# Block compression's first layer by three products of 256 columns for even and odd blocks in place of two of 512

## The chip, the cores and the metric

The kernel runs on one core of one Trainium2 chip. The metric is the device time of one execution in microseconds (us), the median of several runs. Engines are named as in the profile: PE (TensorE; PEld is its loading of weights), DVE (VectorE), ACT (ScalarE), POOL (GpSimd), SP (SyncE, which issues most DMAs).

## What is computed

One inference step of a hybrid decoder layer for 512 prompt tokens and 64 sample tokens (8 requests of 8 tokens, each with 1024 cached rows): an input projection, three mixers, an output projection, a feed-forward part, all in fp32. The change concerns the third mixer's compression of key and value rows to blocks:

```
def compress_blocks(rows, pos_emb, w1, w2):      # CMP_BLOCK 32, CMP_STRIDE 16, CMP_HIDDEN 128
    chunks = rows.reshape(bsz, n_chunks, CMP_STRIDE, g, dh)
    blocks = jnp.concatenate([chunks[:, k:k + n_blocks] for k in range(CMP_SPAN)], axis=2)
    blocks = blocks + pos_emb[:, None, :]
    flat = jnp.transpose(blocks, (0, 1, 3, 2, 4)).reshape(bsz, n_blocks, g, CMP_BLOCK * dh)
    return jax.nn.gelu(flat @ w1) @ w2
```

A block is two neighbouring chunks of 16 rows, so block n is W0 times chunk n plus W1 times chunk n+1, where W0 and W1 are the upper and the lower half of `w1` (1024 x 128 each). It is done for keys (`src` 0) and for values (`src` 1), with 4 heads.

## The kernel before

**Products.** A product in fp32 is made as three products in float32r: each operand is split into a high part (a rounded copy, made by ACT at L93) and a low part (the difference, made by DVE at L96), and high·high, high·low and low·high are added up in PSUM.

**The main stream.** `run_group` (products at L424) runs through the input projection in jobs of 128 output columns: 16 k tiles a job, and 6 products of 288 columns a k tile (`pg<-hhi,whi`, `pg<-hlo,whi`, `pg<-hhi,wlo`, each for two halves of the 576 tokens). Weights are loaded by SP (`raw<-in_w_in`, 256 KB each) and split into `whi` (ACT) and `wlo` (DVE). When a job ends, DVE multiplies the accumulated `pg` into a tile `u` that the job's own tasks then finish (`norm_T` with two fp32 products against `bones`, `kv_finish` with transposes into the staging tiles `tk` and `tks`).

**The side work.** Everything else is in generators that a `Pump` steps through. After each k tile `pump.run` gives it 369 ns per half; each product or transpose that a task issues adds an assumed price (for float32r the larger of 107 ns and columns/2.4 ns). A scheduler then orders the instructions of each engine. The chain of tasks is `compress(0)`, `compress(1)`, then, when the projection's key, value and query jobs are finished, the attention of the sample tokens and of the prompt.

**The compression.** `compress(src)` has 40 units (u, J): for u = 0 to 3 two of the eight requests, 128 rows of chunks (512 columns with the 4 heads), for u = 4 the prompt (32 rows, 128 columns); J = 0 to 7 takes two of a chunk's 16 rows, which is one k tile of W0 and one of W1. A unit's rows are gathered by POOL (`cr`), then `turn(i)` makes them ready: DVE copies them to `by_g` (L692, one buffer), PE transposes four pieces into a tile of `pt` (L124), ACT makes `xh` from it, DVE makes `xl`. Two pairs of `xh` and `xl` take turns. The unit's products follow, two for each of three pairs (weights, rows), where W1's read the rows shifted by one column:

```
            for half in range(2):
                k = half * 8 + J
                for w, x in ((w1h, xh), (w1h, xl), (w1l, xh)):
                    mm(pa[:, :n], w[:, k, :], x[:, half:half + n], start=(J == 0 and first),
                       stop=(J == 7 and half == 1 and w is w1l))
```

They add up in `pa`, the one buffer of `po`. `turn(i + 1)` is issued ahead of the products of unit i. After J = 7 a task `tail` does the rest: `gelu2` with the positions' share `hb` as bias, the second layer and, for keys, a norm (`k_cmp_norm`, with an inverse root `kcr` on POOL). PSUM has three buffers of `pt`, one of `po` and two of `pg`.

**The positions' share.** `prep_w1(src)` loads `w1` in four pieces (`w1r`), splits it into `w1h` and `w1l`, and multiplies each of its 16 k tiles in fp32 by a column of `cols2` (the positions): 16 products, of two records each, with one output row of 128. `compress` copies the row (`hr`) and turns it into the column `hb` by one fp32 product against ones.

Of the kernel before, what the change touches and what calls it, by code (L numbers as in the profile page):

```python
# [76 lines left out]
def hybrid_step_kernel(ctx, tc, x_prompt, x_sample, cache_k, cache_v, cache_win_k, cache_win_v,  # L77
# [11 lines left out]
    def dram(t, off, ap):  # L89
        return bass.AP(tensor=t.tensor, offset=t.offset + off, ap=ap)  # L90
# [67 lines left out]
    def po(name="po"):  # L158
        return psum.tile([128, 512], F32, name=name, tag="o", bufs=1)
# [315 lines left out]
    def kv_finish(br, kv, p, u):  # L475
# [107 lines left out]
    w1, hbs = {}, {}  # L583

    def prep_w1(src):
        w1h = cpool.tile([128, 16, 128], F32R, name="w1h", tag="w1h", bufs=1)
        w1l = cpool.tile([128, 16, 128], F32R, name="w1l", tag="w1l", bufs=1)
        pb = hbs[src] = po()
        for c in range(4):
            raw = cpool.tile([128, 4, 128], F32, name="w1r", tag="cr", bufs=6)  # L590
            nc.sync.dma_start(raw, dram(cmp_w1, src * 2048 * 128 + c * 512 * 128, [[128, 128], [128 * 128, 4], [1, 128]]))
# [4 lines left out]
        w1[src] = w1h, w1l  # L596

    def begin(ci):
        if ci == 1:
# [36 lines left out]

    t1g, t1 = open_pool("t1", side="right")

    def gelu2(hid, pa, hb, n):

        hx = t1.tile([128, 512], F32, name="hx", tag="hx", bufs=1)
        act(hx[:, :n], pa[:, :n], AF.Identity, bias=hb)
        t_ = t1.tile([128, 512], F32, name="ht", tag="ht", bufs=1)
        act(t_[:, :n], pa[:, :n], AF.Square, bias=hb)
        stt(t_[:, :n], t_[:, :n], 1.0 / 0.044715, hx[:, :n], OP.add, OP.mult)
        act(t_[:, :n], t_[:, :n], AF.Tanh, scale=0.7978845608028654 * 0.044715)
        stt(hid[:, :n], t_[:, :n], 1.0, hx[:, :n], OP.add, OP.mult)

    def k_cmp_norm(pc, n):

        kc = t1.tile([128, 256], F32, name="kcn", tag="kcn", bufs=1)
        act(kc[:n], pc[:n, :256])
        sq = t1.tile([128, 256], F32, name="kcs", tag="kcs", bufs=1)
        tt(sq[:n], kc[:n], kc[:n], OP.mult)
        r4 = t1.tile([128, 4], F32, name="kcr", tag="kcr", bufs=1)
        V.reduce_sum(r4[:n], sq[:n].rearrange("p (g d) -> p g d", g=4), axis=AX)
        rsqrt_small(r4[:n], 1.0 / 64)
        tt(kc[:n].rearrange("p (g d) -> p g d", g=4), kc[:n].rearrange("p (g d) -> p g d", g=4),
           r4[:n, :, None].to_broadcast([n, 4, 64]), OP.mult)
        return kc  # L660

    def compress(src):
# [10 lines left out]
        hr = t1.tile([1, 128], F32, name="hr", tag="hr", bufs=1)  # L673
        V.tensor_copy(hr, hbs[src][:1, :128])
        yield
        ps = pt()
        mm(ps[:, :1], hr, ones[:1, :1], start=True, stop=True)
        V.tensor_copy(hb, ps[:, :1])
        pa = None
        X = {}  # L680
        xhl = [[t1.tile([128, 514], F32R, name=f"{n}{k}", tag=f"{n}{k}", bufs=1) for n in ("xh", "xl")] for k in range(2)]
        for t_ in xhl[0] + xhl[1]:
            V.memset(t_[:, 512:514].bitcast(F32), 0.0)

        def turn(i):
            u, J = units[i]
# [9 lines left out]
            act(xh[:, :n], ps[:, :n])  # L696
            tt(xl[:, :n], ps[:, :n], xh[:, :n], OP.subtract)
            if u == 4:
                V.memset(xh[:, n:n + 2].bitcast(F32), 0.0)
                V.memset(xl[:, n:n + 2].bitcast(F32), 0.0)  # L700
            X[i] = (xh, xl)

        for i, (u, J) in enumerate(units):
# [21 lines left out]
            first = True  # L725
            for half in range(2):
                k = half * 8 + J
                for w, x in ((w1h, xh), (w1h, xl), (w1l, xh)):
                    mm(pa[:, :n], w[:, k, :], x[:, half:half + n], start=(J == 0 and first),
                       stop=(J == 7 and half == 1 and w is w1l))  # L730
                    first = False
            yield
            if J < 7:
                continue
            done["tail"] += 1
            pump.add(tail(src, u, n, pa, hb, w2), front=True)
            yield

    def tail(src, u, n, pa, hb, w2):

        gk = cols[:, R_KN:R_KN + 1]
        hid = t1.tile([128, 512], F32, name="hid", tag="hid", bufs=1)
        gelu2(hid, pa, hb, n)
        for _ in range(TY):
            yield
        pc = pt()
# [1206 lines left out]
```

## Time and profile before

| | |
|---|---|
| median of 3 runs | 2938.94 us (2937.56 to 2941.04) |
| profiled execution | 2934.84 us, its span 2933.0 us |
| mean granted clock of PE | 0.994 of full speed |
| PE busy | 2860.9 us (98%) |
| DVE, ACT, POOL busy | 1867.9 (64%), 1157.9 (39%), 585.7 us (20%) |

The span is the profiled part of one execution; the device time of that execution is 1.84 us longer, and 4.10 us below the median of the runs. Busy shares are means over stages with different limits. PE's rows overlap, since a product's row reaches to its modelled end: the price of a product in a stream is the distance from start to start.

### The profile page before, as it was taken

To read this page: it belongs to the slowest core of one execution; us is meant where nothing else is said; L and a number is where in the kernel's file an instruction comes from. 1 tells how busy PE (TensorE), PEld (TensorE's weight loads), DVE (VectorE), ACT (ScalarE), POOL (GpSimd) and SP (SyncE) were. 2 spreads that over 40 slices of the span, in tenths; PEclk is the share of its full clock that TensorE was granted. 3 is DMA by queue.
4 is the path that set the end of the run, shared out by engine and by line. 5 is a ranking of instruction groups with operands and counts; after the bars stand their busy time and mean duration, and the time that the engine had idled before them with its cause. 6 is when DMAs were issued, how large, how long until landed. Compare 5 with 4: busy or idle time off the path is not lost.

```text
span 2933.0 us, 56799 instructions
## 1 busy us (share of the span) xinstructions
PE 2860.9 (98%) x22226; PEld 2739.6 (93%) x22226; DVE 1867.9 (64%) x3790; ACT 1157.9 (39%) x2140; POOL 585.7 (20%) x630
## 2 busy tenths in 40 slices
PE   7999999999999999998999999999999999999999
PEld 6998999888788898998999999999999999999999
DVE  5454445566877747577998888888888753343332
ACT  4353344333555423354544444444444431222222
POOL 3526321664443202033111101101101000000000
PEclk9999999999999999999999999999999999999999
DMA  7434344775231154475553333333333272333333
GB/s 229 126 107 137 103 104 105 223 221 131 60 76 41 50 174 120 132 212 155 174 165 110 110 102 110 111 103 116 100 113 110 79 240 82 116 113 90 89 100 95
DMA packets 467796, 361.94 MB, mean 123 GB/s; under 512 B 64553, under 2 KB 428048, under 8 KB 467528
## 3 DMA queue, kind: packets, MB, share of 16 engines
q1 hardware_dynamic: 443800, 297.89, 34.3%
q0 software_dynamic: 20944, 55.13, 6.5%
q10 hardware_dynamic: 2784, 5.29, 0.5%
q8 instruction: 175, 2.87, 0.4%
q14 instruction: 93, 0.76, 0.1%
HBM read 305.51 MB, written 50.61 MB: 121 GB/s over the span
## 4 chain that ended last, share of the span: by engine, by line
PE 57%; DVE 2%; DMA 1%; issue 1%; ACT 0%; POOL 0%; ACTq 0%; POOLq 0%; DVEq 0%
PE pg L424 24%; PE pg L1833 18%; PE pt L1833 9%; PE po L1833 5%; DVE wlo L96 1%; PE pt L124 1%; PE pt L120 1%; PE pt L424 0%; DVE x L105 0%; DVE X L96 0%; DMA u<-g_d 0%; DVE x L96 0%; DMA raw<-in_w_up_dram 0%; PE po L120 0%; DVE raw L96 0%
## 5 line engine op out<-in xcount | busy, mean ns | idle before, releaser
L93 ACT ACTIVATE whi<-raw 128x512 fp32r<-128x512 f32 x729 | 458.0, 630 | 975.5 <-PE pg L424 673.8
L96 DVE TENSOR_TENSOR wlo<-raw,whi 128x512 fp32r<-128x512 f32 x729 | 506.9, 696 | 398.7 <-ACT whi L93 373.8
L424 PE MATMUL pg<-ghl,whi 128*128 128x288 f32 x2816 | 495.4, 297 | 8.9 <-ACT ghl L93 8.6
L424 PEld LDWEIGHTS pg<-ghl,whi 128*128 128x128 f32 x2816 | 415.2, 189 | 9.9 <-ACT ghl L93 9.0
L424 PE MATMUL pg<-hhi,whi 128*128 128x288 f32 (+1 forms) x1440 | 336.1, 312 | 6.4 <-DVE u L96 4.7
L424 PE MATMUL pg<-hlo,whi 128*128 128x288 f32 (+1 forms) x1440 | 319.6, 300 | 1.1 <-DVE hlo L105 1.1
L424 PE MATMUL pg<-hhi,wlo 128*128 128x288 f32 (+1 forms) x1440 | 314.2, 299 | 0.3 <-DVE wlo L96 0.3
L424 PE MATMUL pg<-ghl,wlo 128*128 128x288 f32 x1408 | 302.3, 296 | 0.0
L424 PEld LDWEIGHTS pg<-hhi,whi 128*128 128x128 f32 (+1 forms) x1440 | 235.0, 190 | 28.5 <-issue 14.3
L1833 PE MATMUL pt<-X,fhi 128*128 128x288 f32 x1280 | 258.5, 296 | 0.0
L1833 PE MATMUL pg<-X,fhi 128*128 128x288 f32 x1232 | 246.7, 294 | 0.0
L424 PEld LDWEIGHTS pg<-hlo,whi 128*128 128x128 f32 (+1 forms) x1440 | 233.4, 189 | 6.3 <-issue 3.1
L424 PEld LDWEIGHTS pg<-hhi,wlo 128*128 128x128 f32 (+1 forms) x1440 | 232.7, 189 | 3.0 <-issue 2.2
L96 POOL TENSOR_TENSOR u<-u 128x576 f32<-128x576 f32 x44 | 69.7, 1584 | 823.8 <-DVE u L96 756.5
L424 PEld LDWEIGHTS pg<-ghl,wlo 128*128 128x128 f32 x1408 | 226.0, 189 | 0.0
L93 ACT ACTIVATE fhi<-wr 128x512 fp32r<-128x512 f32 x225 | 142.2, 632 | 189.4 <-PE pt L1833 107.1
L96 DVE TENSOR_TENSOR flo<-wr,fhi 128x512 fp32r<-128x512 f32 x225 | 197.5, 878 | 13.9 <-ACT fhi L93 11.4
L1833 PEld LDWEIGHTS pt<-X,fhi 128*128 128x128 f32 x1280 | 205.8, 188 | 0.0
L1833 PEld LDWEIGHTS pg<-X,fhi 128*128 128x128 f32 x1232 | 197.8, 188 | 0.0
L424 PE MATMUL pg<-S,whi 128*128 128x288 f32 x1024 | 195.5, 298 | 0.0
L1833 PE MATMUL pt<-X,flo 128*128 128x288 f32 x640 | 189.2, 296 | 0.0
L96 DVE TENSOR_TENSOR x1T<-pg,x1T 128x576 f32<-128x576 f32 x96 | 72.6, 757 | 180.6 <-PE pg L424 180.6
(1308 smaller groups left out, 5756.7 us busy)
## 6 DMA issues: line engine op xcount, KB each, us to landing
wr<-in_w_gate_dram SPq DMA_DIRECT2D x88, 512.0 KB
wr<-in_w_up_dram SPq DMA_DIRECT2D x88, 512.0 KB
raw<-in_w_down_dram SPq DMA_DIRECT2D x176, 256.0 KB
raw<-in_w_in_dram SPq DMA_DIRECT2D x144, 256.0 KB
raw<-in_w_out_dram SPq DMA_DIRECT2D x64, 256.0 KB
g_d<-u POOLq DMA_DIRECT2D x44, 288.0 KB
u<-g_d SPq DMA_DIRECT2D x44, 288.0 KB
raw<-in_w_in_dram SPq DMA_DIRECT2D x64, 128.0 KB
```

Of the source, the lines that this page charges most:

```text
L93: S.activation(out, in_, func, bias=bias, scale=scale, accum_out=accum)
L96: (eng or V).tensor_tensor(out, a, b, op=op)
L120: PE.matmul(out, lhsT, rhs, start=start, stop=stop, skip_group_check=True, **kw)
L124: PE.transpose(out, in_, ident)
L424: PE.matmul(ps[:m, s, :HALF], w[:, k, :m], x[:, s * HALF:(s + 1) * HALF], start=(k0 + k == 0 and n == 0), stop=(k0 + k == n_k - 1 and n == 2))
L1833: PE.matmul(P[n], w[:, k, :], xx, start=(j == 0 and q_ == 0), stop=(j == 7 and q_ == 2))
```

## The change

For u < 4 the blocks are taken in pairs. With chunk n of a unit written as x(n), the block at an even place 2m is W0·x(2m) + W1·x(2m+1), which is W0·(x(2m) − x(2m+1)) + (W0+W1)·x(2m+1); the block at the odd place is W1·(x(2m+2) − x(2m+1)) + (W0+W1)·x(2m+1). So three products of 256 columns stand for two of 512, each still three times for the split parts: 9 products of 256 columns a unit where there were 6 of 512. Of the parts that serve this:

- `turn` for u < 4: from the transposed rows in `pt` ACT copies the odd columns into a new tile `by_d` (256 columns); DVE writes the differences even − odd (256 and 255 columns) to it; ACT makes `xh` in two pieces (256 odd columns straight from `pt`, 511 differences from `by_d`), DVE makes `xl` in the same two pieces. `by_d` shares the one buffer of `by_g`, so the next unit's `by_g` comes behind this unit's last `xl`.
- Products: `pa` collects W0's and W1's parts in its two halves, `pb` the shared part with `wsh` and `wsl` (W0+W1, split). `pb` is a tile of `pt`, held for the eight units of one u.
- `compress` loads the pieces of `w1` a second time (four more loads of 256 KB for each `src`, by SP), adds W0 and W1 on DVE and splits the sum.
- The positions' share: 32 products of two columns for each `src` (`w1h` against the high and low part of the positions, `w1l` against the high part and zero), in place of the fp32 products; DVE adds the two columns to `hb`.
- To make room: `tk` and `tks` get one buffer in place of two; `gelu2` works in `hid` and `hx` alone (an addition on DVE brings in `pb`), and `k_cmp_norm` uses the buffers of `hx` and `hid`.

For u = 4 the six products of 128 columns remain. The diff, cut to its core:

```diff
-            stage[br, kv] = [t1.tile([128, 4, 256], F32, name="tk", tag="tk", bufs=2),
-                             t1.tile([TS, 256], F32, name="tks", tag="tks", bufs=2) if not (kv and br) else Vs[:, br - 1, :], 0]
+            stage[br, kv] = [t1.tile([128, 4, 256], F32, name="tk", tag="tk", bufs=1),
+                             t1.tile([TS, 256], F32, name="tks", tag="tks", bufs=1) if not (kv and br) else Vs[:, br - 1, :], 0]
...
-        pb = hbs[src] = po()
...
-            for k in range(4):
-                j = 4 * c + k
-                mm(pb[:1, :128], cols2[:, src * 16 + j:src * 16 + j + 1], raw[:, k, :], start=(j == 0), stop=(j == 15))
...
+        if pb is None:
+            act(hx[:, :n], pa[:, :n], AF.Identity, bias=hb)
+        else:
+            act(hid[:, :256], pb[:, :256], AF.Identity, bias=hb)
+            tt(hx.rearrange("p (n e) -> p e n", e=2), pa.rearrange("p (e n) -> p e n", e=2),
+               hid[:, None, :256].to_broadcast([128, 2, 256]), OP.add)
...
-        mm(ps[:, :1], hr, ones[:1, :1], start=True, stop=True)
...
+        for c in range(2):
+            a, b = [cpool.tile([128, 4, 128], F32, name="w1r", tag="cr", bufs=6) for _ in range(2)]
+            w1_in(a, src, c)
+            w1_in(b, src, c + 2)
+            yield
+            yield
+            tt(a, a, b, OP.add)
+            split(wsh[:, 4 * c:4 * c + 4], wsl[:, 4 * c:4 * c + 4], a)
         ps = pt()
+        for j in range(16):
+            mm(ps[:, :2], w1h[:, j, :], pos[:, j, 0:2], start=(j == 0), stop=False)
+            mm(ps[:, :2], w1l[:, j, :], pos[:, j, 2:4], start=False, stop=(j == 15))
+        V.reduce_sum(hb, ps[:, :2], axis=AX)
...
+                eo = ps.rearrange("p (n e) -> p e n", e=2)
+                d_ = t1.tile([128, 512], F32, name="by_d", tag="by_g", bufs=1)
+                act(d_[:, 256:], eo[:, 1])
+                tt(d_[:, :256], eo[:, 0], d_[:, 256:], OP.subtract)
+                tt(d_[:, 256:511], eo[:, 0, 1:], d_[:, 256:511], OP.subtract)
+                act(xh[:, 512:], eo[:, 1])
+                act(xh[:, :511], d_[:, :511])
+                tt(xl[:, 512:], eo[:, 1], xh[:, 512:].bitcast(F32), OP.subtract)
+                tt(xl[:, :511], d_[:, :511], xh[:, :511].bitcast(F32), OP.subtract)
...
-                pa = po()
+                pa, pb = po(), pt() if u < 4 else None
...
+                for w_, k, out, x0 in (((w1h, w1l), J, pa[:, :256], 0), ((w1h, w1l), 8 + J, pa[:, 256:512], 256),
+                                       ((wsh, wsl), J, pb[:, :256], 512)):
+                    for n_, (w, x) in enumerate(((w_[0], xh), (w_[0], xl), (w_[1], xh))):
+                        mm(out, w[:, k, :], x[:, x0:x0 + 256], start=(J == 0 and n_ == 0 and x0 != 256),
+                           stop=(J == 7 and n_ == 2))
```

How the instructions stand on PE now. Before, a unit of the compression, from its turn's transposes on: three rows of the main stream (L424, each two products), then the unit's six products.

```order
L124 MATMUL pt<-ident,by_g 128x128 x4
L424 MATMUL pg<-hhi,whi 128x288 x2
L424 MATMUL pg<-hlo,whi 128x288 x2
L424 MATMUL pg<-hhi,wlo 128x288 x2
L120 MATMUL po<-xh_789,w1h 128x512
L120 MATMUL po<-xl_790,w1h 128x512
L120 MATMUL po<-xh_789,w1l 128x512
L120 MATMUL po<-xh_789,w1h 128x512
L120 MATMUL po<-xl_790,w1h 128x512
L120 MATMUL po<-xh_789,w1l 128x512
```

In the changed order the same engine, at the place where u = 3, J = 3 and 4 of the keys are turned (main product 768 of the projection); `bones` is the fp32 product of a job's norm, `pt<-xh,wsh` is the share of W0+W1.

```order
L124 MATMUL pt<-ident,by_g 128x128 x4
L120 MATMUL pt<-u,bones 128x288 x2
L120 MATMUL pt<-xh_888,wsh 128x256
L120 MATMUL pt<-xl_889,wsh 128x256
L120 MATMUL po<-xh_888,w1h 128x256
L120 MATMUL pt<-xh_888,wsl 128x256
L120 MATMUL po<-xl_889,w1h 128x256
L120 MATMUL po<-xh_888,w1l 128x256
L120 MATMUL po<-xh_888,w1h 128x256
L120 MATMUL po<-xl_889,w1h 128x256
L124 MATMUL pt<-ident,by_g 128x128 x4
L120 MATMUL po<-xh_888,w1l 128x256
```

Between the two rows of `by_g` transposes no product of the main stream is left. Counted over the whole order, 4 products of the main stream at the least, and mostly 12 to 24, stand between the transposes of successive turns before; after the change 15 to 33 for most sample units, but at main product 672 (u = 2, J = 3 to 6) 9, 0 and 0, and at 768 (u = 3, J = 2 to 5) 11, 0 and 6, and for the units of u = 4 mostly 0 to 6 (0, 6, 2, 1, 0, 0, 0 for keys). In all PE has 20863 instructions before and 21085 after (384 products of 512 columns less, 576 of 256 more), DVE 3792 and 4004, ACT 2013 and 2147, SP 1074 and 1082, POOL 635 in both. The attention's first product stands behind main product 2049 in both; the compression's last instructions on PE stand behind about main product 1450 before, about 1640 after.

On DVE, before the change, two turns of the compression, from one copy into `by_g` to the copy two turns later:

```order
L692 COPY by_g<-cr 128x2x4x64
L96 TENSOR_TENSOR xl_790<-pt,xh_789 128x512
L96 TENSOR_TENSOR wlo<-raw,whi 128x512
L692 COPY by_g<-cr 128x2x4x64
L96 TENSOR_TENSOR xl_792<-pt,xh_791 128x512
L692 COPY by_g<-cr 128x2x4x64
```

and from one copy to the next in the changed order:

```order
L711 COPY by_g<-cr 128x2x4x64
L96 TENSOR_TENSOR by_d<-pt,by_d 128x256
L96 TENSOR_TENSOR by_d<-pt,by_d 128x255
L96 TENSOR_TENSOR wlo<-raw,whi 128x512
L96 TENSOR_TENSOR xl_889<-pt,xh_888 128x256
L96 TENSOR_TENSOR xl_889<-by_d,xh_888 128x511
L711 COPY by_g<-cr 128x2x4x64
```

The one pass over 512 columns (`xl<-pt,xh`) has become four, of 256, 255, 256 and 511 columns, and all of them stand between two copies into `by_g`.

## Rows read from the trace of the kernel before

**Rows 1.** The page's head and its first part: the span, then busy time (share of the span) and number of instructions of an engine.
```profile
span 2933.0 us, 56799 instructions
...
PE 2860.9 (98%) x22226; PEld 2739.6 (93%) x22226; DVE 1867.9 (64%) x3790; ACT 1157.9 (39%) x2140; POOL 585.7 (20%) x630
```

**Rows 2.** The table of windows, three of 100 us that cover the compression of rows: busy time (and instructions) of PE, PEld, DVE, ACT and POOL, the granted clock of PE, the share of the DMA engines, GB/s.
```profile
100.00:200.00 100.00, 99.52 (x662) 92.21 (x661) 49.29 (x91) 45.93 (x75) 38.74 (x41) 1.00 0.39 113
200.00:300.00 100.00, 98.72 (x690) 89.83 (x689) 49.19 (x118) 36.77 (x72) 49.11 (x49) 1.00 0.45 130
300.00:400.00 100.00, 100.00 (x693) 93.13 (x692) 44.02 (x98) 40.00 (x71) 23.33 (x33) 1.00 0.33 83
```

**Rows 3.** The waits of PE from 70 to 500 us: what PE waited for, us in total, times, longest.
```profile
PE pt L124 <- DVE kcn L96: 0.7, 1, 0.7
PE pt L124 <- DVE tk L493: 0.6, 1, 0.6
PE pt L124 <- DVE u L105: 0.3, 1, 0.3
PE pt L120 <- DVE sc L96: 0.2, 1, 0.2
```

**Rows 4.** PE's timeline, the products of one unit of the compression (512 columns) and the first products of the main stream behind them. Columns: start, us from first start to last end of the row, engine, line, what, number of records.
```profile
208.83 0.40 PE L120 MATMUL po<-xh,w1h 128*128 128x512 f32 x1
209.06 0.40 PE L120 MATMUL po<-xl,w1h 128*128 128x512 f32 x1
...
210.23 0.43 PE L424 MATMUL pg<-hhi,whi 128*128 128x288 f32 x2
210.49 0.42 PE L424 MATMUL pg<-hlo,whi 128*128 128x288 f32 x2
```

**Rows 5.** PE's timeline at 725 us (attention, not the compression): products of 256 columns in float32r.
```profile
725.10 0.28 PE L120 MATMUL pt<-kl,qhl 128*128 128x256 f32 x1
725.22 0.28 PE L120 MATMUL pt<-kh,qhl 128*128 128x256 f32 x1
725.34 0.28 PE L120 MATMUL pt<-kl,qhl 128*128 128x256 f32 x1
```

**Rows 6.** PE's timeline at 215 us: the second and the sixth of the six products of one prompt unit (128 columns).
```profile
215.25 0.27 PE L120 MATMUL po<-xl,w1h 128*128 128x128 f32 x1
...
215.69 0.28 PE L120 MATMUL po<-xh,w1l 128*128 128x128 f32 x1
```

**Rows 7.** PE's timeline at 54 us: products for the positions' share, in fp32 (`w1r` against a column of `cols2`), and the row behind them.
```profile
54.44 2.78 PE L120 MATMUL po<-w1r,cols 128*1 128x128 f32 x24
57.15 0.54 PE L424 MATMUL pg<-hhi,whi 128*128 128x288 f32 x2
```

**Rows 8.** The timeline of all engines, one turn of a unit: the copy into `by_g`, its four transposes, the split into `xh` and `xl`.
```profile
241.48 0.43 DVE L692 COPY by_g<-cr 128x512 f32<-128x512 f32 x1 [0.43 <-PE pt L124]
...
241.96 0.66 PE L124 MATMUL pt<-ident,by_g 128*128 128x128 f32 x4
...
242.71 0.60 ACT L93 ACTIVATE xh<-pt 128x512 fp32r<-128x512 f32 x1 [0.58 <-PE pt L124]
...
243.34 0.69 DVE L96 TENSOR_TENSOR xl<-pt,xh 128x512 fp32r<-128x512 f32 x1 [0.15 <-ACT xh L93]
```

**Rows 9.** Groups of instructions by line and form from 60 to 1000 us: busy time in total, mean ns of one | idle time of the engine before them.
```profile
L96 DVE TENSOR_TENSOR wlo<-raw,whi 128x512 fp32r<-128x512 f32 x150 | 104.3, 696 | 87.6 <-ACT whi L93 65.0 <-PE pt L124 22.4
L96 DVE TENSOR_TENSOR xl<-pt,xh 128x512 fp32r<-128x512 f32 x64 | 44.0, 687 | 7.9 <-ACT xh L93 7.7
L93 ACT ACTIVATE xh<-pt 128x512 fp32r<-128x512 f32 x64 | 38.2, 597 | 80.3 <-PE pt L124 79.5
L93 ACT ACT_TABLE_LOAD x24 | 30.8, 1283 | 0.4
L493 DVE COPY tk<-pt 128x512 f32<-128x512 f32 x12 | 8.2, 680 | 0.1
L96 POOL TENSOR_TENSOR kcr<-kcr,mhalf 128x4 f32<-128x4 f32 x4 | 4.2, 1038 | 29.5 <-DVE kcr L102 29.5
L96 DVE TENSOR_TENSOR s<-s,pt 128x256 f32<-128x256 f32 x8 | 3.4, 420 | 18.7 <-PE pt L120 18.7
L93 ACT ACTIVATE pcT<-pt 128x256 f32<-128x256 f32 x8 | 3.0, 370 | 1.2 <-PE pt L124 1.2
```

**Rows 10.** The waits of DVE from 70 to 400 us: us in total, times, longest.
```profile
DVE kcn L96 <- POOL kcr L96: 11.7, 5, 6.6
DVE xl L96 <- ACT xh L93: 9.8, 38, 1.4
```

**Rows 11.** The table of windows around two places where PE stood still: columns as in Rows 2.
```profile
24.50:27.70 3.20, 0.71 (x7) 0.51 (x5) 0.69 (x1) 0.00 (x0) 0.00 (x0) 1.00 1.07 379
27.70:34.50 6.80, 5.58 (x24) 5.12 (x23) 2.68 (x4) 4.64 (x9) 0.00 (x0) 0.50 1.05 320
700.00:705.00 5.00, 2.81 (x22) 2.57 (x20) 4.28 (x11) 0.63 (x1) 4.87 (x8) 1.00 1.31 256
705.00:710.00 5.00, 4.00 (x20) 4.03 (x21) 4.35 (x7) 1.20 (x2) 4.78 (x8) 0.69 1.52 233
```

**Rows 12.** The first layer's products by the view of one tile (`xh`): duration min/median/max in ns, then the start of the first and of the last, in us.
```profile
L120 PE MATMUL po<-xh,w1h x160: 219/396/500, 72.4 to 397.1; 128*128 128x512 f32 x128, 128*128 128x128 f32 x32
```

**Rows 13.** PE's timeline where the sample tokens' attention begins: its first products (`eqb`).
```profile
487.08 0.39 PE L120 MATMUL pt<-eqb,L 64*128 64x8 f32 x2
```

More of the change, by code (lines that the diff above doesn't have):

```diff
@@ L587, in prep_w1, with w1_in @@
         w1l = cpool.tile([128, 16, 128], F32R, name="w1l", tag="w1l", bufs=1)
[L588 removed]
         for c in range(4):
             raw = cpool.tile([128, 4, 128], F32, name="w1r", tag="cr", bufs=6)
[L591 removed]
+            w1_in(raw, src, c)
             split(w1h[:, 4 * c:4 * c + 4], w1l[:, 4 * c:4 * c + 4], raw)
[L593 to L595 removed]
         w1[src] = w1h, w1l
+    def w1_in(raw, src, c):
+        nc.sync.dma_start(raw, dram(cmp_w1, src * 2048 * 128 + c * 512 * 128, [[128, 128], [128 * 128, 4], [1, 128]]))
     def begin(ci):
@@ L672, in compress @@
         hb = t1.tile([128, 1], F32, name="hb", tag="hb", bufs=2)
-        hr = t1.tile([1, 128], F32, name="hr", tag="hr", bufs=1)
-        V.tensor_copy(hr, hbs[src][:1, :128])
+        wsh, wsl = [t1.tile([128, 8, 128], F32R, name=n, tag=n, bufs=1) for n in ("wsh", "wsl")]
+        pos = t1.tile([128, 16, 4], F32R, name="pos", tag="pos", bufs=1)
+        p16 = cols2[:, src * 16:src * 16 + 16]
+        V.memset(pos[:, :, 3].bitcast(F32), 0.0)
+        act(pos[:, :, 0], p16)
+        V.tensor_copy(pos[:, :, 2], pos[:, :, 0].bitcast(F32))
+        tt(pos[:, :, 1], p16, pos[:, :, 0].bitcast(F32), OP.subtract)
+        for c in range(2):
[6 more added lines that the diff above has]
+            split(wsh[:, 4 * c:4 * c + 4], wsl[:, 4 * c:4 * c + 4], a)
+        ps = pt()
+        for j in range(16):
+            mm(ps[:, :2], w1h[:, j, :], pos[:, j, 0:2], start=(j == 0), stop=False)
+            mm(ps[:, :2], w1l[:, j, :], pos[:, j, 2:4], start=False, stop=(j == 15))
+        V.reduce_sum(hb, ps[:, :2], axis=AX)
         yield
-        ps = pt()
-        mm(ps[:, :1], hr, ones[:1, :1], start=True, stop=True)
-        V.tensor_copy(hb, ps[:, :1])
-        pa = None
+        pa = pb = None
         X = {}
-        xhl = [[t1.tile([128, 514], F32R, name=f"{n}{k}", tag=f"{n}{k}", bufs=1) for n in ("xh", "xl")] for k in range(2)]
+        xhl = [[t1.tile([128, 768], F32R, name=f"{n}{k}", tag=f"{n}{k}", bufs=1) for n in ("xh", "xl")] for k in range(2)]
         for t_ in xhl[0] + xhl[1]:
-            V.memset(t_[:, 512:514].bitcast(F32), 0.0)
+            V.memset(t_[:, 510:512].bitcast(F32), 0.0)
         def turn(i):
@@ L695, in turn @@
             xh, xl = xhl[i % 2]
-            act(xh[:, :n], ps[:, :n])
-            tt(xl[:, :n], ps[:, :n], xh[:, :n], OP.subtract)
             if u == 4:
+                act(xh[:, :n], ps[:, :n])
+                tt(xl[:, :n], ps[:, :n], xh[:, :n], OP.subtract)
                 V.memset(xh[:, n:n + 2].bitcast(F32), 0.0)
                 V.memset(xl[:, n:n + 2].bitcast(F32), 0.0)
+            else:
+                eo = ps.rearrange("p (n e) -> p e n", e=2)
[7 more added lines that the diff above has]
+                tt(xl[:, :511], d_[:, :511], xh[:, :511].bitcast(F32), OP.subtract)
             X[i] = (xh, xl)
@@ L722, in compress @@
             if J == 0:
-                pa = po()
+                pa, pb = po(), pt() if u < 4 else None
             xh, xl = X.pop(i)
[L725 to L731, printed above, removed]
+            if u < 4:
+                for w_, k, out, x0 in (((w1h, w1l), J, pa[:, :256], 0), ((w1h, w1l), 8 + J, pa[:, 256:512], 256),
[3 more added lines that the diff above has]
+                           stop=(J == 7 and n_ == 2))
+            else:
+                first = True
+                for half in range(2):
+                    k = half * 8 + J
+                    for w, x in ((w1h, xh), (w1h, xl), (w1l, xh)):
+                        mm(pa[:, :n], w[:, k, :], x[:, half:half + n], start=(J == 0 and first),
+                           stop=(J == 7 and half == 1 and w is w1l))
+                        first = False
             yield
@@ L735, in compress, with tail @@
             done["tail"] += 1
-            pump.add(tail(src, u, n, pa, hb, w2), front=True)
+            pump.add(tail(src, u, n, pa, pb, hb, w2), front=True)
             yield
-    def tail(src, u, n, pa, hb, w2):
+    def tail(src, u, n, pa, pb, hb, w2):
         gk = cols[:, R_KN:R_KN + 1]
         hid = t1.tile([128, 512], F32, name="hid", tag="hid", bufs=1)
-        gelu2(hid, pa, hb, n)
+        gelu2(hid, pa, pb, hb, n)
         for _ in range(TY):
```

18 lines of the change are left out of this document (8 added, 10 removed).

## The prediction

> **What bounds the kernel now.** I read the page's head first: PE is busy for 98% of the span, DVE for 64% [rows 1]. That is a mean, so the second view is the table of windows over the stage that the change touches: from 100 to 400 us PE is busy for 98.7 to 100 us of each 100, at a granted clock of 1.00, while DVE has 44 to 49 us and ACT 37 to 46 us of work [rows 2]. The third view is PE's waits: from 70 to 500 us PE waited for named work 1.8 us in all [rows 3]. So here every product costs its place in PE's stream and nothing else; a product less is time gained, and a wait that appears on PE is time lost, since nothing is there now. The fourth view is the turn of a unit in the timeline, which tells how long the other engines need to make a unit ready. What ends the stage is not the compression: its last first-layer product starts at 397.1 us [rows 12] and the attention at 487.08 us [rows 13], and in the changed order the attention's first product still stands behind main product 2049. Compression that ends later within this order therefore costs nothing by itself. What counts is PE's work and PE's stops in the stage.
>
> **What the change saves on PE.** Products of 512 columns follow each other at 0.233 us: six of them from 208.83 to 210.23, which is 1.40 us [rows 4]. Products of 256 columns in float32r stand in attention at 0.120 us from start to start [rows 5]. A sample unit thus goes from 6 x 0.233 = 1.40 to 9 x 0.120 = 1.08 us, 0.32 us less; 4 u x 8 J x 2 `src` are 64 units: **20.4 us less**. The price per column hardly differs; the gain is the quarter of the columns that goes (3072 to 2304 a unit).
>
> The positions' share: 64 fp32 records go. 24 of them took 54.44 to 57.15 us, 0.113 each [rows 7], so 7.2 us. 64 products of two columns come. No row shows such a product in a stream; the nearest is the 128-column product at 0.11 us [rows 6], since each also needs a 128 x 128 weight load, so 7.0 us. I take 0 for the difference; the bounds are ±3.
>
> Work that lies beside PE: four more weight pieces a `src` on SP, their additions and splits on DVE and ACT (some 4 us each in all a `src`), and per sample unit on DVE two passes of about 256 columns from PSUM (0.42 us each by the nearest form, `s<-s,pt` 128x256) and `xl` in two pieces, on ACT one pass of 256 more (0.37, `pcT<-pt`) [rows 9]. DVE gets about 1.2 us a unit, 77 us in some 330; with 44 to 49 us of 100 busy it has room for that as a share [rows 2]. Its order is the problem.
>
> **What the change adds as stops.** Before, the copy into `by_g` for the next unit needed only the four transposes of this one. Now `by_d` lies in the same buffer, so the next copy comes behind this unit's last `xl`. I worked the loop out by hand. From the copy's start to the transposes 0.48 us, from these to ACT 0.75 us [rows 8]: 1.23. ACT's odd columns 0.37, DVE's two differences 0.42 each, with 0.05 for each hand-over: 2.5. ACT's 511 columns 0.60, DVE's `xl` of 511 columns 0.69 [rows 9]: about **3.9 us from copy to copy**; where PE takes the last five products ahead of the next transposes, 4.2. A `wlo` of the main stream that stands in between adds up to 0.70, an evacuation `tk` 0.68, a load of ACT's table 1.28 [rows 9]. The passes now read every other column of PSUM; no row shows what that costs. If it cost as much as the full width (0.69 in place of 0.42 for DVE's two, 0.60 in place of 0.37 for ACT's), the loop would be 4.7.
>
> This loop is harmless wherever PE has as much other work between two turns. Pairs of main products cost 0.26 us [rows 4], transposes 0.109 each; with the counts of the changed order most units have 3.9 to 5.5 us of PE work between turns. Not so in these places; the value taken, then the bounds:
>
> - main product 672 (9, 0 and 0 main products between turns): 2.6, 2.7 and 2.2 us of work against 4.2, and a norm's table load and `tk` stand in the loop on top: 8 us (5 to 10).
> - main product 768 (11, 0, 6): in the order shown 2.4 us of work (eight products, four fp32 records of `bones` at 0.25, four transposes), its neighbours 3.8 and 2.9: 6 us (3.5 to 8).
> - some 18 units with 3.8 to 4.1 us of work: a tenth or two each, 3 us (0 to 8, the latter with strided reads at full price).
> - u = 4: small turns, 1.1 to 2.6 us of work against a loop of about 1.7 (copy 0.42, transposes and hand-over 0.65, ACT and DVE 0.28 each): 3 us (0 to 6).
> - start of `compress(0)`: the sums of W0 and W1 must be loaded and split before the first products: 3 us (0 to 5). Start of `compress(1)`: DVE has some 8 us queued in front of the first `xl` against 5 of PE work: 3 us (0 to 4).
> - the norm of the keys: DVE already waits 11.7 us for POOL's `kcr`, up to 6.6 at a time [rows 10], and stands in front of the next unit's `xl`; before, PE had main products meanwhile: 2 us (0 to 6).
> - the clock: after PE stood still for 2.5 of 3.2 us, the next 6.8 us ran at 0.50; after a pause of 3.2 us at 700 the next 5 us had 0.69 [rows 11]. 5.6 busy us at half speed are 2.8 lost. The new stops are mostly single microseconds: 2 us (0 to 10, three such places).
>
> The sum taken is **30 us** (8.5 to 57). With 20.4 saved the change is +9.6. The profiled execution would go from 2934.84 to 2944.4; it stood 4.1 below the median, and against the median of 2938.94 this is 2948.5, of which I forecast **2948 us**. Bounds of the sum: 2927 to 2975. A measurement can tell 0.2%, 5.9 us, from no change.
>
> **Rivals.**
>
> 1. *The saving counts, the stops don't come* (faster). For it: PE now waits 1.8 us in 430 [rows 3], ACT waits and DVE waits are all for PE or for things off the path, and the loop of 3.9 is below the work between most turns. Against: the two blocks have no main product to run, whatever the loop's exact size. With 8.5 us of stops 2927 us. It decides below 14.5 us of stops: 22%.
> 2. *Stops and saving cancel*, 14.5 to 26.3 us of stops: the blocks cost as taken, the small items nothing. 14 + 6 gives 2938.5: 28%.
> 3. *The loop sets the stage* (slower than forecast): with strided reads at full price and a `wlo` in half of the turns, 4.7 + 0.3 = 5.0 us for each of 64 units against some 4.5 of work: 32 us of stops plus 14 in the two blocks, 2938.9 - 20.4 + 46, about 2965 or over. For it: DVE's idle time in a loop can't be used by others in an in-order engine. Against: 0.26 us for reading strided is assumed, not seen. 5%.
> 4. *The price of a product hangs on its number, not its columns* (the change wouldn't do what it says). From 128 to 288 columns the price only goes from 0.11 to 0.132 us [rows 4, 6], since each product reloads its weights; at 0.132 a product of 256 saves 0.21 us a unit, 13.4 in all: 2955 us. The rows at 0.120 [rows 5] speak against it: 2%. The Trainium skill has a stronger form of it (TensorE: Matmul & The Clock Gate, section on the back-to-back issue gap): a stream of load and product pairs takes about 81 ns at 128 columns and 131 ns at 512. By a straight line between these, an estimate, nine of 256 would take 0.88 us and six of 512 0.79, and the change would lose 6 us on PE instead of winning 20. This trace does not agree: 512 columns take 233 ns and 256 take 120 [rows 4, 5].
>
> The forecast itself, stops from 26.3 us up to 45, has 43%. Faster by over 0.2% is 0.22, within 0.2% 0.28, slower 0.50 (43 + 5 + 2). **The range** is 2926 to 2964: below, the smallest sum of stops; above, the forecast's case with the clock's cost or the strided reads in it, but not both at their ends. The likeliest case has 2945 to 2964 for itself.
>
> **What would show it.** Right: in 70 to 450 us PE's waits grow from 2 to 20 or 40 us, named for ACT `xh`, DVE `xl`, `by_g` or `by_d`, most of it in two places of 5 to 10 us where no product of line 424 stands; products of 256 columns at 0.120; DVE busy some 60 to 80 us longer, PE busy some 20 shorter; attention behind the same main product, with the stage from 70 to 487 longer by the change in time. Wrong: PE's waits below 10 us (rival 1); 256 columns at 0.13 or more (rival 4); passes from PSUM at 0.6 us for 256 columns (rival 3); or a difference that arises behind 500 us, where I expect none.

## The result, and the profile after

| | before | after |
|---|---|---|
| median | 2938.43 us (2937.56 to 2941.04) | 2980.7 us (2979.82 to 2982.27) |
| ratio | 1 | 1.0143 (1.0125 to 1.016) |
| profiled span | 2933.0 us | 2978.3 us |
| attention's first product | 487.08 us | 535.38 us |

The change costs 42 us; the forecast was 10, and its range ended at 2964 us. All of it arises before the attention of the sample tokens: its first product (`eqb`, [rows 13]) is 48.3 us late, and the span ends 45.3 us late.

```profile
535.38 0.39 PE L120 MATMUL pt<-eqb,L 64*128 64x8 f32 x2
```

The page's head (beside [rows 1]): PE has 21 us more busy time, although it has less to do.

```profile
span 2978.3 us, 57578 instructions
...
PE 2881.6 (97%) x22414; PEld 2762.9 (93%) x22414; DVE 1954.6 (66%) x4002; ACT 1199.7 (40%) x2274; POOL 584.1 (20%) x630
```

The same three windows as in [rows 2], with the same columns: PE is down to 93.6 and 86.7 of 100 us, and from 200 to 300 us its granted clock is 0.78 of full speed (a mean: the clock rows of these traces hold 1.00 and 0.50 alone).

```profile
100.00:200.00 100.00, 93.60 (x671) 87.21 (x670) 65.59 (x138) 45.83 (x97) 40.87 (x44) 0.97 0.37 104
200.00:300.00 100.00, 86.70 (x514) 78.85 (x513) 55.44 (x138) 45.69 (x91) 27.57 (x29) 0.78 0.37 106
300.00:400.00 100.00, 99.85 (x756) 95.44 (x756) 66.76 (x135) 41.62 (x92) 39.17 (x40) 1.00 0.43 109
```

Where that is, by shorter windows: the places at main product 672 (170 to 195 us) and 768 (210 to 235), the units of u = 4 of the keys (240 to 280), the start of the values (290 to 300) and their end (470 to 480). Columns as in [rows 2].

```profile
170.00:195.00 25.00, 18.93 (x109) 16.14 (x109) 15.31 (x34) 12.86 (x25) 10.31 (x12) 0.86 0.32 91
210.00:235.00 25.00, 18.86 (x98) 16.22 (x97) 13.59 (x29) 11.96 (x23) 2.54 (x3) 0.73 0.24 69
240.00:250.00 10.00, 7.76 (x56) 6.60 (x54) 5.50 (x16) 7.43 (x14) 0.00 (x0) 0.99 0.27 74
250.00:260.00 10.00, 9.88 (x47) 9.05 (x47) 5.46 (x20) 3.34 (x9) 1.92 (x3) 0.50 0.36 106
260.00:270.00 10.00, 10.00 (x45) 8.82 (x45) 4.99 (x21) 3.50 (x9) 0.17 (x1) 0.50 0.30 87
270.00:280.00 10.00, 9.77 (x63) 8.99 (x63) 7.30 (x15) 8.19 (x15) 7.34 (x7) 0.82 0.49 141
290.00:300.00 10.00, 6.47 (x37) 6.08 (x38) 5.21 (x11) 3.44 (x8) 3.90 (x4) 0.83 0.38 105
470.00:480.00 10.00, 5.98 (x35) 5.16 (x35) 4.70 (x10) 9.71 (x14) 7.87 (x8) 0.92 0.48 134
```

In the first two PE lacks 6.1 us each (it stands still for so long), at clocks of 0.86 and 0.73. **From 250 to 270 us PE lacks 0.1 us and has a clock of 0.50**: 47 and 45 records in 10 us, where the full windows of 300 to 400 us have about 76. One wait stands ahead of it, at 247.8 to 250.1 us:

```profile
247.44 0.35 PE L424 MATMUL pg<-hlo,whi 128*128 128x288 f32 x1
250.12 0.47 PE L120 MATMUL po<-xh,w1h 128*128 128x128 f32 x1 [2.34 <-ACT xh L93]
```

At another place the clock falls while PE is busy without a break: behind the 32 two-column products of the positions' share, which stand at 70.9 to 74.3 us.

```profile
68.89:75.72 6.83, 6.83 (x59) 6.83 (x59) 3.44 (x14) 1.34 (x4) 4.15 (x5) 1.00 0.64 191
75.72:79.13 3.41, 3.41 (x16) 3.40 (x15) 0.69 (x1) 0.06 (x1) 1.63 (x2) 0.50 0.61 178
```

The first five of PE's waits from 70 to 500 us (as [rows 3], where there were 1.8 us):

```profile
PE po L120 <- ACT xh L93: 6.9, 2, 4.5
PE pt L120 <- ACT u L93: 6.8, 4, 4.0
PE pt L120 <- ACT xh L93: 3.5, 4, 2.0
PE pt L124 <- DVE u L105: 3.1, 3, 1.8
PE pt L124 <- DVE by_g L711: 1.9, 2, 1.6
```

To add it up I took, from 60 us to the attention, each product's distance to the next start. "PE work" is the first quartile of these distances for products of one form, times their number (0.131 us for 288 columns, 0.1185 for 256). What lies above it is split, by windows of 5 us: the time in which PE is idle is "stops", its busy time times (1 - clock) is "half clock", and the rest is "short gaps". Another choice of the forms moves "PE work" and "short gaps" by 1 to 2 us against each other.

| kernel | attention at | PE work | stops | half clock | short gaps | ratio to before |
|---|---|---|---|---|---|---|
| before | 487.1 | 408.7 | 2.0 | 0.0 | 16.0 | 1 |
| after | 535.4 | 390.0 | 26.5 | 26.6 | 31.9 | 1.0143 |
| r13, the changed kernel again | 536.9 | 389.4 | 26.7 | 29.3 | 31.2 | 1.0154 (1.0137 to 1.0171) |
| r14, order alone | 501.2 | 388.1 | 19.0 | 6.4 | 27.5 | 1.0039 (1.0028 to 1.0050) |
| r15, buffer alone | 506.2 | 389.1 | 12.6 | 16.2 | 27.4 | 1.0047 (1.0030 to 1.0064) |
| r17, order, buffer, start | 486.5 | 390.0 | 12.6 | 4.6 | 18.5 | 0.9947 (0.9933 to 0.9960) |
| r16, before with rows of u = 4 | 503.9 | 409.1 | 6.3 | 12.9 | 15.3 | 1.0052 (1.0035 to 1.0069) |

From before to after: -18.7 + 24.5 + 26.6 + 15.9 = 48.3 us.

Measured beside r13 to r16 the kernel before took 2939 us; beside the other runs it took 3035 to 3048 us, and there PE stopped in the attention of the sample tokens while less data moved. From 490 to 690 us, r16 and then r8 (both the kernel before in that stage):

```profile
490.00:690.00 200.00, 199.84 (x2239) 170.65 (x2238) 119.51 (x343) 67.73 (x123) 118.89 (x117) 1.00 0.69 206
```

```profile
490.00:690.00 200.00, 160.38 (x1504) 130.26 (x1499) 78.69 (x224) 44.99 (x81) 88.01 (x91) 0.85 0.51 151
```

So the expectations' microseconds, made against 2939, are read as ratios, and the stage up to the attention is compared by its own trace. The changed kernel itself has 1.0143, 1.0154 (r13) and 1.0085 (r6): ratios that were not measured together can differ by 0.7% for one kernel, more than their intervals say.

### The profile page after: what moved, and what is told of

It reads as the page before. It is cut to its first block, busy times and chain, and to the rows that moved or that the text cites. A ratio compares the mean times of both kernels' runs of the same rounds, so it can differ in the third digit from the quotient of the medians.

```text
span 2978.3 us, 57578 instructions
## 1 busy us (share of the span) xinstructions
PE 2881.6 (97%) x22414; PEld 2762.9 (93%) x22414; DVE 1954.6 (66%) x4002; ACT 1199.7 (40%) x2274; POOL 584.1 (20%) x630
## 4 chain that ended last, share of the span: by engine, by line
PE 56%; DVE 2%; DMA 1%; issue 0%; ACT 0%; POOL 0%; SPq 0%; ACTq 0%; DVEq 0%; POOLq 0%
PE pg L424 23%; PE pg L1871 17%; PE pt L1871 9%; PE po L1871 5%; PE pt L424 1%; DVE wlo L96 1%; PE pt L124 1%; PE pt L120 0%; DMA u<-g_d 0%; DVE x L105 0%; DMA raw<-in_w_out_dram 0%; DVE X L96 0%; DVE x L96 0%; DMA raw<-in_w_up_dram 0%; PE po L120 0%
## 5 line engine op out<-in xcount | busy, mean ns | idle before, releaser
L424 PE MATMUL pg<-ghl,whi 128*128 128x288 f32 x2816 | 495.4, 297 | 9.4 <-ACT ghl L93 8.8
L424 PEld LDWEIGHTS pg<-ghl,whi 128*128 128x128 f32 x2816 | 415.0, 189 | 10.6 <-ACT ghl L93 9.3
L424 PE MATMUL pg<-hhi,whi 128*128 128x288 f32 (+1 forms) x1440 | 338.4, 311 | 7.6 <-DVE u L96 6.4
L424 PE MATMUL pg<-hlo,whi 128*128 128x288 f32 (+1 forms) x1440 | 331.9, 304 | 3.0 <-DVE hlo L105 2.8
L424 PE MATMUL pg<-hhi,wlo 128*128 128x288 f32 (+1 forms) x1440 | 322.5, 302 | 0.3 <-DVE wlo L96 0.3
L424 PE MATMUL pg<-ghl,wlo 128*128 128x288 f32 x1408 | 302.3, 296 | 0.0
L424 PEld LDWEIGHTS pg<-hhi,whi 128*128 128x128 f32 (+1 forms) x1440 | 236.3, 192 | 22.5 <-issue 15.7
L424 PEld LDWEIGHTS pg<-hlo,whi 128*128 128x128 f32 (+1 forms) x1440 | 239.1, 191 | 8.6 <-DVE hlo L105 3.9
L424 PEld LDWEIGHTS pg<-hhi,wlo 128*128 128x128 f32 (+1 forms) x1440 | 236.7, 191 | 3.4 <-issue 2.2
L424 PEld LDWEIGHTS pg<-ghl,wlo 128*128 128x128 f32 x1408 | 226.0, 189 | 0.0
L424 PE MATMUL pg<-S,whi 128*128 128x288 f32 x1024 | 195.5, 298 | 0.0
```

The costliest lines, as they stand in the source:

```text
L424: PE.matmul(ps[:m, s, :HALF], w[:, k, :m], x[:, s * HALF:(s + 1) * HALF], start=(k0 + k == 0 and n == 0), stop=(k0 + k == n_k - 1 and n == 2))
```

## The experiments

Theory A: the loss comes from the stretches in which the changed order leaves PE no main products, by stops and by the half clock that goes with them. B: the long loop of `by_g` and `by_d` costs in every unit. C: the split into nine products itself costs. D: the two-column products cost.

**r13 and r6: the changed kernel again.** r13 has 1.0154 (1.0137 to 1.0171), r6 1.0085 (1.0061 to 1.011); r6 has 29.3 us of stops and 27.2 of half clock before the attention, so the same stage.

> The changed kernel, unchanged, as the base on the chip of this call. All theories: 0.8 to 1.5% slower than the kernel before; attention starts 40 to 50 us later than in the kernel before's first trace, with some 27 us of stops and 27 us of half clock from 60 us to there.

> The changed kernel, unchanged, on the chip that runs the experiments of this call. All theories: 1.2 to 1.6% slower than the kernel before, with 25 us or so of stops and as much of half clock before the attention starts.

**r14 and r2: the order alone.**

```diff
+            pump.cost += 1000.0 if u < 4 else 1000.0
             yield
             if J < 7:
```

> The changed kernel with 1000 ns more charged for each unit, on one chip with the changed kernel itself. A (stretches without main products): attention starts 25 us or more before the changed kernel's, half clock under 10 us, and the ratio is lower by 0.6 points or more. B (the loop in every unit): within 10 us of the changed kernel.

> The changed kernel with each unit of the compression charged 1000 ns more by the pump, so that the same work is spread over more main products: at least 8 stand between any two turns (0 before), mostly 18 to 30, and the compression ends at main product 2004 in place of about 1640. No instruction is added or taken away. A: the three empty stretches and the one at the end of the values go, with their 18 us of stops and 22 us of half clock: 2938 to 2945 us; what stays is the start and some 0.23 us per unit of short gaps. B: the loop is the same and costs the same in each unit: 2965 to 2980. C: 2975 to 2985.

r14 is 36 us faster than r13, measured beside it, with the same instructions. Of the half clock 23 us go, of the stops 8. The same kernel as r2 gave 1.0033 (1.0019 to 1.0048), about 10 us over the kernel before, where A had 0 to 7. From 170 to 280 us, r13 and then r14:

```profile
170.00:280.00 110.00, 95.25 (x557) 85.59 (x556) 66.12 (x162) 56.42 (x110) 28.48 (x30) 0.80 0.32 91
```

```profile
170.00:280.00 110.00, 105.97 (x807) 100.46 (x806) 70.25 (x168) 52.00 (x109) 22.61 (x25) 1.00 0.44 115
```

PE lacks 14.8 us at a clock of 0.80 in the one, 4.0 us at 1.00 in the other. B, which expected r14 within 10 us of r13, falls as the main cause, and so does C, which had r2 as slow as the changed kernel.

**r15 and r3: the buffer alone.** The room for it comes from the pool of gathered rows, 5 buffers in place of 6 wherever that pool is used.

```diff
-            raw = cpool.tile([128, 2, 256], F32, name="cr", tag="cr", bufs=6)
+            raw = cpool.tile([128, 2, 256], F32, name="cr", tag="cr", bufs=5)
...
-                d_ = t1.tile([128, 512], F32, name="by_d", tag="by_g", bufs=1)
+                d_ = t1.tile([128, 512], F32, name="by_d", tag="by_d", bufs=1)
```

> The changed kernel with a buffer of its own for by_d, on one chip with the changed kernel. B: attention starts 25 us or more before the changed kernel's. A: the buffer alone gives little, since the units are then packed closer (ends at main product 1308) and PE stops in other places: within 10 us of the changed kernel, half clock 15 to 25 us.

> The changed kernel with a buffer of its own for by_d (the buffer comes from the pool of gathered rows, 5 in place of 6), so that the next copy into by_g waits for the transposes only, as before the change. All operations stay. A: the order becomes another one (1 to 9 us of PE work between turns, the compression ends at main product 1308), no stretch of several turns without main products: 2925 to 2945 us. B: the loop falls from 4.2 to about 2.7 us: 2920 to 2930. C: over 2965.

r15 is 32 us faster than r13, so A's forecast of little was wrong here, and B's was right: 14 us of stops go. But 13 us of the half clock go too, and 16 stay, some 5 of them from 170 to 280 us:

```profile
170.00:280.00 110.00, 104.75 (x758) 97.94 (x757) 73.36 (x179) 57.05 (x119) 42.20 (x43) 0.95 0.46 128
```

The same kernel as r3 gave 1.0070 (1.0049 to 1.0091), outside what A, B and C had said. The order changes with the buffer (the compression ends at main product 1308), so this run is not the loop alone, and it does not part A from B: in the empty stretches it is the loop's length that makes PE stop.

**r7: order and buffer** (the 1000 ns of r14 and the edit of r15).

> The changed kernel with both edits at once: by_d in a buffer of its own (gathered rows 5 buffers in place of 6) and 1000 ns more charged for each unit. Between two turns stand mostly 18 to 30 main products, 10 at the least after the first, and the nine products of a unit follow each other. A (stretches without cover, and the clock): the stops nearly go, what stays is the start of each source: 10 us faster to 3 us slower than the kernel before. B (the loop in each unit): the same or better, 5 to 15 us faster. C (the split into nine products itself): 20 us or more slower.

r7 has 0.9997 (0.9985 to 1.0008), as A forecast; C falls again. Up to the attention it has 14.5 us of stops, 8.0 of half clock and 18.1 of short gaps. Neither edit alone brings the short gaps below 27; both together bring them near the 16 of before.

**r9, r10 and r17: the starts as well.** To the buffer of r15 and 850 ns a unit come four steps ahead of each source's first turn. r10 and r17 are one kernel; r9 also has the old fp32 products for the positions' share.

```diff
+        for _ in range(4):
+            pump.cost += 1500.0
+            yield
         pa = pb = None
...
+            pump.cost += 850.0 if u < 4 else 850.0
```

> The changed kernel with four edits: by_d in a buffer of its own, 850 ns more charged for each unit, four steps of 1500 ns charged between the sums of W0 and W1 and the first turn of each source (so that main products cover the splits), and the positions' share made by the old fp32 products. At least 12 main products stand between turns but for the first, the compression ends at main product 1950. A: the three places that still stopped in the run of two edits (both starts and the end of the keys, about 14 us with their clock) go for the most part: 5 to 14 us faster than the kernel before. B (each unit's loop): 5 us faster to equal. C (the nine products): 10 us or more slower.

> As the run before, but with the change's own positions' share (32 products of two columns per source). D (these products, which come in one stretch with nothing beside them, bring the half clock with them): 3 to 8 us slower than the run before. If only their number counts: equal within 3 us.

> The changed kernel with by_d in a buffer of its own, 850 ns more charged for each unit and four steps of 1500 ns ahead of the first turn of each source; the change's own positions' share. A: the 19 us of PE work that the change saves are kept but for 6 to 10 us at the two starts and in units of u = 4: 6 to 14 us faster than the kernel before, half clock under 6 us. B: equal to 5 us faster. C: 10 us or more slower.

r9 has 0.9984 (0.9973 to 0.9995), r10 0.9984 (0.9973 to 0.9996), r17 0.9947 (0.9933 to 0.9960). So this version is faster than the changed kernel, at 1.0085 to 1.0154, by 1 to 2%. Against the kernel before it is 0.2 to 0.5% ahead, but that this is the products' saving isn't shown: r9 came out at the edge between what A and B had, one kernel gives two values whose intervals don't meet, and in r17's trace the attention starts at 486.5 us, only 0.6 us before the 487.1 of the kernel before. What the traces do show is that the loss is gone from the stage: the longest single wait of PE in r17 from 70 to 480 us is 1.3 us.

D falls as the main cause: r9 and r10 are equal. But its mechanism is there. In the changed kernel the clock is at 0.50 for 3.4 us behind each of the two rows of two-column products, at 76 and at 284 us, together 3.4 us lost; r10 has both (at 74 and 282 us), r17 none behind its first.

**r16: rows of small units in the kernel before.**

```diff
                 V.memset(xl[:, n:n + 2].bitcast(F32), 0.0)
+                pump.cost -= 268.0
...
+            if u == 4:
+                pump.cost -= 640.0
+                pump.debt += 200.0
             yield
```

> The kernel before, with the units of u = 4 charged nothing, so that they stand in a row with 0 main products between most turns, as in the changed kernel (1.1 us of PE work from turn to turn), twice, once per source. These units use no by_d and are not changed. A: the clock falls to half in or behind these rows as it does in the changed kernel at 250 to 275 us, and the stops of the small turns come too: attention starts 8 to 20 us later than in the kernel before. B: no more than 3 us.

r16 is 14.7 us slower with no part of the change in it. Windows, then PE's timeline where the clock falls:

```profile
210.00:220.00 10.00, 9.67 (x78) 8.62 (x76) 5.63 (x24) 4.09 (x10) 1.03 (x1) 0.95 0.39 107
220.00:230.00 10.00, 10.00 (x51) 9.05 (x51) 4.66 (x19) 3.98 (x11) 6.56 (x6) 0.53 0.34 100
230.00:240.00 10.00, 10.00 (x77) 8.25 (x76) 5.41 (x13) 3.42 (x7) 7.40 (x8) 1.00 0.39 119
385.00:395.00 10.00, 10.00 (x53) 9.47 (x52) 3.34 (x20) 2.05 (x7) 1.52 (x9) 0.57 0.13 26
```

```profile
218.01 0.27 PE L120 MATMUL po<-xl,w1h 128*128 128x128 f32 x1
218.12 0.28 PE L120 MATMUL po<-xh,w1l 128*128 128x128 f32 x1
...
219.64 0.63 PE L124 MATMUL pt<-ident,by_g 32*128 32x32 f32 x4
...
220.47 0.41 PE L120 MATMUL po<-xl,w1h 128*128 128x128 f32 x1
220.69 0.41 PE L120 MATMUL po<-xh,w1l 128*128 128x128 f32 x1
```

Products of 128 columns come 0.11 us apart at 218 us and 0.22 from 220 us on. In the 10 us ahead of the two falls, at 219 and 386 us, PE stood still for 0.3 and 0.1 us. These two rows make 10.2 of the 12.9 us of half clock; the other 2.7 stand at the end of a wait of 5.1 us, at 251 us, and behind it; the edit brought that too. B, which gave 3 us, can't explain the rows.

**r1 and r18: the old turn.** It leaves out the odd copy and the differences, so the result is not the layer's; r18 also has the old fp32 products and 900 ns more a unit.

```diff
-                act(d_[:, 256:], eo[:, 1])
...
+                act(xh[:, :n], ps[:, :n])
+                tt(xl[:, :n], ps[:, :n], xh[:, :n], OP.subtract)
...
-                                       ((wsh, wsl), J, pb[:, :256], 512)):
+                                       ((wsh, wsl), J, pb[:, :256], 128)):
```

> The changed kernel with the old turn: ACT and DVE split the transposed 512 columns as they are, in one piece each; no odd copy, no differences (so the output is not the layer's). The 9 products of 256 columns, pb, the sums of W0 and W1, the new bias and the single tk stay. Theory A (stretches): the loss comes from the places where the changed order has no main products to cover the making of the operands, by stops of PE and by the half clock after them; with the short turn these stretches are not there: 2920 to 2930 us, PE waits under 5 us from 70 to 500 us, clock 1.00 there. Theory B (loop): every unit loses by the long loop from copy to copy: the same 2920 to 2930. Theory C (products): the split into 9 products, the tile pb held in pt and the extra weights are to blame: over 2960 us.

> The changed kernel with the old turn (no odd copy, no differences, so the output is not the layer's), the positions' share by the old fp32 products, and 900 ns more charged for each unit: the nine products of 256 columns alone, fully covered. A and B: 14 to 20 us faster than the kernel before, what the products can save at most. C: less than 8 us.

r1 has 0.9989 (0.9970 to 1.0008), r18 0.9983 (0.9966 to 1.0001). C falls by r1, which has all of the changed products. A and B missed in both: the 14 to 20 us that the products could win did not show. Up to the attention r18 has 35.6 us of stops, 9.8 of them one wait for `xl` at the start of the values, and r1 27.6 us of stops and 17.2 of half clock.

**r4, r11, r12, r8: single parts.** r4 is the kernel before with the new positions' share, r11 the changed kernel with the old one, r12 the kernel before with one buffer for `tk` and `tks`, r8 the kernel before with 700 ns more a unit. (r5, the kernel before once more for its trace, met one wait of 13.5 us of its own and had the attention at 512.4 us.)

> The kernel before with one part of the change alone: the positions' share by 32 products of two columns per source from the split weights. A, B and C: within 3 us of the kernel before, 2936 to 2942. If the bias products or their order at the start cost by themselves (rival D): 2943 to 2950.

> The changed kernel with the positions' share made by the old fp32 products; nothing else undone, though the order shifts: the empty stretches are still there (0, 0, 0 and 0, 0 main products between turns of the keys, 0 to 1 at the end of the values). A: as slow as the changed kernel, 20 to 40 us over the kernel before on this chip. D: 5 to 10 us better than that.

> The kernel before with one buffer for tk and for tks, as in the change; its order of PE's instructions is that of the kernel before. A, B, C: no difference, within 3 us. If the single buffer makes the evacuation wait for the store (rival R): 5 us or more slower.

> The kernel before with 700 ns more charged for each unit, so that its compression is spread over as many main products (ends at 1914) as in the run that combines both edits. A, B and C: no difference from the kernel before, within 4 us: there the units are covered already. If spreading by itself is worth time (rival E), it is 6 us or more faster.

r4 has 1.0015 (1.0003 to 1.0028), which would allow D its smallest value, r11 1.0121 (1.0101 to 1.0142), r12 0.9989 (0.9975 to 1.0003), r8 0.9985 (0.9969 to 1.0001). The single `tk` costs nothing that shows, spreading alone brings nothing that can be told from zero, and with the old positions' share the changed kernel stays slow.

## Why the prediction was wrong

- **PE's saving: right.** 20.4 us were forecast, 18.7 measured. The sign named for it was wrong: PE's busy time did not shrink by 20 us but grew by 21, since a product at half the clock is busy for longer. Products of 256 columns come 0.12 us apart, as [rows 5] said (PE's timeline; the first three rows are explained below):

```profile
110.54 0.42 PE L424 MATMUL pg<-hhi,whi 128*128 128x288 f32 x2
110.94 0.38 PE L120 MATMUL pt<-xh,wsh 128*128 128x256 f32 x1
111.16 0.43 PE L424 MATMUL pg<-hlo,whi 128*128 128x288 f32 x2
...
112.95 0.28 PE L120 MATMUL po<-xh,w1h 128*128 128x256 f32 x1
113.07 0.28 PE L120 MATMUL po<-xl,w1h 128*128 128x256 f32 x1
113.19 0.28 PE L120 MATMUL po<-xh,w1l 128*128 128x256 f32 x1
113.31 0.29 PE L424 MATMUL pg<-hhi,wlo 128*128 128x288 f32 x1
```

- **Positions' share: right in the products' price, without the clock.** The 32 products of one source, from the second to the last 30 steps in 3.35 us, 0.11 each; the 3.4 us of half clock behind the two rows had no price:

```profile
70.88 0.25 PE L120 MATMUL pt<-pos,w1l 128*128 128x2 f32 x1
...
74.23 0.25 PE L120 MATMUL pt<-pos,w1l 128*128 128x2 f32 x1
```

- **Passes on every other column of PSUM: right, at the lower bound.** 0.42 us on DVE and 0.38 on ACT, as for the contiguous rows of [rows 9]; rival 3's premise falls. Groups by line and form, 60 to 540 us:

```profile
L96 DVE TENSOR_TENSOR by_d<-pt,by_d 128x256 f32<-128x256 f32 x64 | 27.1, 424 | 70.4 <-ACT by_d L93 70.4
L93 ACT ACTIVATE by_d<-pt 128x256 f32<-128x256 f32 x64 | 24.6, 384 | 125.4 <-PE pt L124 125.4
```

- **DVE's extra work: right.** 77 us forecast, 86.7 measured (1867.9 to 1954.6 in [rows 1] and the page above).
- **Stops: right in size, mostly right in place.** Without the clock the sum was 28 us, measured were 24.5 more: 6.1 (8 taken) and 6.1 (6 taken) in the two stretches, 2.6 in the units of u = 4 (3), 4.5 in one wait at the start of the values (3). That the sum fits so well is in part luck: the 4.0 at the end of the values were not listed, and of the 3 for units below the loop and the 2 for the norm of the keys nothing shows as stops. The loop is the one worked out by hand, with a load of ACT's table in it; all engines at 179 us, from one turn's transposes to the next copy into `by_g`:

```profile
178.77 1.05 PE L124 MATMUL pt<-ident,by_g 128*128 128x128 f32 x4
...
179.91 0.38 ACT L93 ACTIVATE by_d<-pt 128x256 f32<-128x256 f32 x1 [2.78 <-PE pt L124]
180.32 1.28 ACT L93 ACT_TABLE_LOAD   x1
180.33 0.88 DVE L96 TENSOR_TENSOR by_d<-pt,by_d 128x256 f32<-128x256 f32 x2 [2.01 <-ACT by_d L93]
...
182.01 0.38 ACT L93 ACTIVATE xh<-pt 128x256 fp32r<-128x256 f32 x1
...
182.27 0.63 ACT L93 ACTIVATE xh<-by_d 128x511 fp32r<-128x511 f32 x1
...
182.94 0.69 DVE L96 TENSOR_TENSOR xl<-by_d,xh 128x511 fp32r<-128x511 f32 x1
...
183.66 0.43 DVE L711 COPY by_g<-cr 128x512 f32<-128x512 f32 x1
```

- **Half clock: the step that failed.** I took 2 us (0 to 10) from the two places of [rows 11], where PE had stood still for 2.5 and 3.2 us, and so priced the clock by stops. Measured were 26.6 us: 2.4 in the first stretch, 4.8 in the second, 11.9 from 245 to 275 us, 2.9 at the start of the values, 4.7 in three dips at 76, 461 and 478 us. About 10 us of it stand between or right behind PE's stops, as priced, but at six places and not the three of the upper bound. The largest part fell on units of u = 4 standing in a row. A wait of 2.3 us stands ahead of it, and by the places of [rows 11] this would cost some 3 us; but the clock stayed at 0.50 until 274 us, through a row of small products in which PE did not stop. I had put a price on the stops of these units and none on their clock. r16 makes such rows in the kernel before and loses 10.2 us of clock in them with no such wait ahead; r14 keeps all instructions, puts main products between the turns, and 23 us of half clock go. The Trainium skill (TensorE: Matmul & The Clock Gate, section on the second failure mode by cycling of the PSUM queue) tells of a kernel in bf16 whose clock swings between its two levels because PE idles for very short moments between groups of products. The rows at 250 to 270 us show no such moments (their 0.1 us of idle time is the end of that wait), and the clock stays down. Whether moments that the profile doesn't show or the small products themselves bring the clock down, no run here separates.
- **Short gaps: a term missing from the sum.** 15.9 us, 0.25 per sample unit. The rows at 110 us above show one: the pair before `pt<-xh,wsh` should end its turn after 0.26 us, the product comes after 0.40, and the next after 0.22 in place of 0.12. In the changed order the first product of a unit stands just where ACT's `xh` is due, with main products behind it. The nearest term of my sum was the 3 us (0 to 8) for units below the loop. In r14 and r15 27 us are left, in r7 and r17 18: it takes a shorter loop and more cover at once. That each such product pays for being issued at the moment its operand arrives is argued from these rows, not shown by a run.

So rival 1 (no stops) and rival 4 (price by number) were wrong. Rival 2 (stops and saving cancel) would fit the 24.5 us of stops, had they come without the clock. The time is where rival 3 had it, at 2965 or over, but not for its reason, since the passes cost no more than taken. The forecast's mechanism, stops in stretches without main products, held for the stops, and the sign was right. What failed is the price of the clock, and a term for the short gaps was missing: stops and saving as measured would have left a loss of 6 us; half clock and short gaps added 42.

## What to carry to other kernels

Where PE is the bound and side work is woven into it, ask of each stretch what PE does there, not only whether it waits: a row of small products here cost half the clock for 10 to 24 us at a time. A change that makes units cheaper on PE and dearer on DVE and ACT needs the order's price for a unit to be raised, or cover is lost where it is most needed. One shared buffer, as that of `by_g` and `by_d`, can make the next unit wait for all of this unit's passes and not for the first of them alone.

## What was not expected of the hardware

The clock stood at 0.50 over 20 us in which PE shows 19.9 us busy, and in r16 it fell twice with no more than 0.3 us of idle time in the 10 us ahead. Products of two columns with a full weight load take 0.11 us, no less than those of 128 columns. Reading every other column of PSUM costs nearly the same as reading them side by side (424 ns against 420 on DVE, 384 against 370 on ACT, for 256 columns).
